# A hybrid flow-matching step: the DRAM round of the triangular blocks in 1 KB pieces on two queues, and small elementwise work moved to GpSimd

## The chip, the cores and the metric

One core of a Trainium2 chip runs the whole program in one launch. The metric is the device time of one execution in microseconds (us), the median of several runs. The core has a matrix engine (TensorE, PE in the profile; its weight loads are PEld), a vector engine (VectorE, DVE), an activation engine (ScalarE, ACT), GpSimd (POOL) and SyncE (SP), whose only work here is to issue DMAs. ScalarE and GpSimd can issue DMAs too. Each engine works through its own instructions in a fixed order and waits on semaphores.

## The reference, cut to what matters

Two layers. Each has four token mixers side by side on 512 latent and 128 context tokens (640 rows, width 1024), which share one input and one output projection, and then a SwiGLU channel mixer.

```python
z = einsum('bld,de->ble', modulated_norm(x), p['w_in'])          # combined input projection
# gated DeltaNet, per chunk of 64 tokens, 4 heads, 2 directions:
a   = where(strict, einsum('nbhid,nbhjd->nbhij', kb, kc) * dmask, 0.0)
sol = lax.linalg.triangular_solve(a + eye(c), rhs, lower=True, unit_diagonal=True)
u, w = sol[..., :dv], sol[..., dv:]
def step(s, xs):                                                 # scan over the chunks
    v_new = u_i - w_i @ s;  o_i = qd_i @ s + qk_i @ v_new
    s = s * gl_i + kd_i.T @ v_new
# GQA: q, k = rms_norm per head, then rope_2d: x*cos + swap(x)*sin
# MLA: q = rms_norm(zcq) @ wq_up;  ckv = rms_norm(zckv);  k_rope = rope_2d(zkr)
x = x + mods[2] * (concat([o_gqa, o_na, o_dn, o_mla]) @ p['w_out'])
x = x + mods[5] * ((silu(h @ w_gate) * (h @ w_up)) @ w_down)
```

All of it is float32. The kernel's products with weights are made of three passes: each weight tile is cast to a rounded form `whi` by ScalarE, and the rest, `wlo = w - whi`, is a subtraction of two tiles in SBUF; the matmuls are `whi*hi`, `whi*lo` and `wlo*hi`.

## The kernel before, in words

A layer is the *mixer* stage (`_Build.mixer`) and then the channel mixer. In the mixer, TensorE's order is written out by a planner (`_Order`): generators `yield` the time from which their next TensorE work may run, and the planner picks by rank. The numbers in `od.via(...)` and `od.now + ...` are the planner's estimates of how long the other engines or a DMA take; nothing else depends on them. The order on the other engines and the DMA queues is set by a scheduler when the program is built.

The planner interleaves two kinds of work. The **filler** is the input projection (tiles `acc` and `tacc`, weights through `weights`, L309) and in layer 0 small `mpart` products for the modulation, whose weights `wmd` come on SP's queue. The **delta chain** (`delta_chain`) is a long chain of small steps: Gram matrices of the keys give 20 blocks of 64x64 per direction (`self.M`, tile `dM`); their diagonal 16x16 blocks are inverted (`inverse16`); from these the 64x64 inverses are put together by TensorE (`inverse`, tiles `ivr`, `invp`, `ivy`); then ten chunks are scanned (`scan`, tiles `ks`, `qs`, `ysp`, `spp`, `opp`), and `delta_out` (tiles `dno`, `otp`) ends it. Only then does the attention begin.

`inverse16` needs another layout: one block per partition instead of one row per partition. So the diagonal blocks go **through DRAM** (`dinv`): eight DMAs write them (L1025, pieces of 64 bytes), two loads bring one direction each into `ivx` and `ivw` (L1034 and L1035, 40 partitions of 4 KB), VectorE transposes one of them (L1037) and does 60 short products and differences on 104 partitions (L1044, L1048), two DMAs write the result back (L1051, L1052) and eight bring it to `rt` (L1055). All 20 are issued by SP. VectorE's copy L1037 waits for the second load, and whatever stands behind it in VectorE's order waits too.

On VectorE there are also: `wlo` of every weight (L309), the copies of `rt` into `dM` (L1128), the last two steps of the GQA rotary (L1441, L1442; GpSimd makes `gsw`, the swapped product, before them), and the scaling of the MLA rows `mcr` (L1552), which are read back from DRAM (`dcraw`) into a single buffer, one of five row blocks at a time.

`wst`, the staging tile of a weight, has three buffers, `whi` and `wlo` two each.

## Time and profile before

| | |
|---|---|
| three runs | 1982.02, 1990.4 and 2092.3 us, median 1990.4 |
| the profiled execution | 1986.23 us, its span 1984.5 us |
| busy in the span | PE 1855.4, DVE 1098.1, ACT 734.1, POOL 282.7 us |
| mean granted TensorE clock | 0.97 of full speed |
| layer 0 | mixer about 45 to 520 us, channel mixer to 1040 us |
| layer 1 | mixer about 1040 to 1480 us, channel mixer to the end |

A row of a chain or a timeline begins with its start in us from the span's start and its length in us. A timeline row with x3 merges three like instructions that follow each other; what stands in brackets is the idle time of the engine before it, and what ended that. The granted clock is a share of full speed (2.4 GHz), averaged over a stretch; at any moment it is full or half.

### The profile page before, as it was taken

To read this page: it belongs to the slowest core of one execution; us is meant where nothing else is said; L and a number is where in the kernel's file an instruction comes from. 1 tells how busy PE (TensorE), PEld (TensorE's weight loads), DVE (VectorE), ACT (ScalarE), POOL (GpSimd) and SP (SyncE) were. 2 spreads that over 40 slices of the span, in tenths; PEclk is the share of its full clock that TensorE was granted. 3 is DMA by queue.
4 is the path that set the end of the run, shared out by engine and by line. 5 is a ranking of instruction groups with operands and counts; after the bars stand their busy time and mean duration, and the time that the engine had idled before them with its cause. 6 is when DMAs were issued, how large, how long until landed. Compare 5 with 4: busy or idle time off the path is not lost.

```text
span 1984.5 us, 40378 instructions
## 1 busy us (share of the span) xinstructions
PE 1855.4 (93%) x16620; PEld 1751.5 (88%) x16620; DVE 1098.1 (55%) x2372; ACT 734.1 (37%) x1505; POOL 282.7 (14%) x470
## 2 busy tenths in 40 slices
PE   5998998899999999999999889789999999999997
PEld 4976787778899999999989889677889999999997
DVE  6464646677657547647555674567765232333344
ACT  4622133766442212222345223277655221221231
POOL 1120312233310000000032131223322000000001
PEclk8998798999999999999999899899999999999999
DMA  7344333132535536435423222223352222222221
GB/s 295 128 114 122 112 94 104 30 108 73 165 130 167 158 99 191 150 113 188 131 89 109 57 76 70 74 56 75 90 172 80 77 78 79 75 67 83 74 96 54
DMA packets 116521, 213.51 MB, mean 108 GB/s; under 512 B 44401, under 2 KB 64369, under 8 KB 116209
## 3 DMA queue, kind: packets, MB, share of 16 engines
q1 hardware_dynamic: 113520, 206.22, 33.3%
q0 software_dynamic: 2816, 4.72, 1.2%
q8 instruction: 130, 2.13, 0.4%
q14 instruction: 55, 0.44, 0.1%
HBM read 186.29 MB, written 19.89 MB: 104 GB/s over the span
## 4 chain that ended last, share of the span: by engine, by line
PE 77%; DVE 8%; DMA 6%; ACT 4%; issue 2%; SPq 2%; POOL 1%; DVEq 0%; ACTq 0%; POOLq 0%
PE acc L351 56%; PE tacc L351 7%; PE ptp L363 2%; PE sc L351 2%; PE pvo L351 2%; PE invp L351 1%; DVE wlo L309 1%; DMA wst<-wout 1%; PE mpart L351 1%; DMA ivw<-dinv 1%; ACT p L1288 1%; ACT whi L308 1%; PE ysp L351 1%; PE spp L351 1%; SPq L1705 1%
## 5 line engine op out<-in xcount | busy, mean ns | idle before, releaser
L351 PE MATMUL acc<-h,whi 128*128 128x256 f32 (+1 forms) x3520 | 685.0, 313 | 2.6 <-ACT h L574 1.4
L351 PEld LDWEIGHTS acc<-h,whi 128*128 128x128 f32 x3520 | 582.6, 190 | 12.4 <-issue 5.1
L308 ACT CAST whi<-wst 128x1024 fp32r<-128x1024 f32 (+3 forms) x210 | 203.6, 970 | 714.6 <-PE acc L351 664.9
L351 PE MATMUL acc<-h,wlo 128*128 128x256 f32 (+1 forms) x1760 | 414.7, 313 | 7.7 <-DVE wlo L309 7.7
L309 DVE TENSOR_TENSOR wlo<-wst,whi 128x1024 fp32r<-128x1024 f32 (+3 forms) x210 | 237.8, 1133 | 210.7 <-ACT whi L308 209.8
L351 PEld LDWEIGHTS acc<-h,wlo 128*128 128x128 f32 x1760 | 322.6, 191 | 10.8 <-DVE wlo L309 8.8
L351 PE MATMUL acc<-g,whi 128*128 128x256 f32 (+1 forms) x1128 | 216.6, 309 | 0.0
L351 PEld LDWEIGHTS acc<-g,whi 128*128 128x128 f32 x1128 | 185.9, 188 | 0.1
L541 POOL TENSOR_TENSOR sq<-sq 128x256 f32<-128x256 f32 (+1 forms) x48 | 48.6, 1012 | 926.2 <-ACT sq L535 925.8
L1806 DVE SCALAR_TENSOR_TENSOR x<-acc,mods,x 128x256 f32<-128x256 f32 (+1 forms) x144 | 55.6, 434 | 186.5 <-PE acc L351 186.4
L507 DVE SCALAR_TENSOR_TENSOR wmj<-wmd,cb 128x1024 f32<-128x1024 f32 x112 | 136.8, 1221 | 39.6 <-DMA wmd<-wmodT 38.4
L351 PE MATMUL tacc<-whi,h 128*128 128x256 f32 (+1 forms) x640 | 149.3, 316 | 1.5 <-ACT whi L308 1.5
L351 PE MATMUL acc<-g,wlo 128*128 128x384 f32 (+1 forms) x564 | 135.2, 309 | 0.0
L351 PEld LDWEIGHTS tacc<-whi,h 128*128 128x128 f32 x640 | 111.5, 195 | 10.5 <-issue 5.0
L351 PE MATMUL acc<-oh,whi 128*128 128x384 f32 (+1 forms) x512 | 115.1, 315 | 1.9 <-DVE xe L1806 1.9
L363 PE MATMUL ptp<-cbase,p 128*128 128x128 f32 x512 | 81.4, 284 | 29.6 <-ACT p L1288 12.3
L351 PEld LDWEIGHTS acc<-g,wlo 128*128 128x128 f32 x564 | 103.2, 188 | 0.0
L351 PE MATMUL tacc<-wlo,h 128*128 128x256 f32 (+1 forms) x320 | 98.9, 309 | 1.8 <-DVE wlo L309 1.8
L363 PEld LDWEIGHTS ptp<-cbase,p 128*128 128x128 f32 x512 | 57.0, 142 | 45.9 <-ACT p L1288 17.1
L2122 DVE TENSOR_TENSOR sg<-acc,sg 128x256 f32<-128x256 f32 x88 | 39.1, 485 | 101.9 <-PE acc L351 101.9
L1288 ACT ACTIVATE p<-sc,sm 128x768 f32<-128x768 f32 (+1 forms) x96 | 79.8, 831 | 33.4 <-DVE sm L1285 23.9
L351 PEld LDWEIGHTS acc<-oh,whi 128*128 128x128 f32 x512 | 84.7, 190 | 4.5 <-PE acc L351 2.4
(322 smaller groups left out, 2624.8 us busy)
## 6 DMA issues: line engine op xcount, KB each, us to landing
wmd<-wmodT SPq DMA_DIRECT2D x56, 512.0 KB, 4.3
wst<-wg SPq DMA_DIRECT2D x44, 512.0 KB, 3.6
wst<-wu SPq DMA_DIRECT2D x44, 512.0 KB, 3.6
wmd<-wmod SPq DMA_DIRECT2D x40, 512.0 KB, 6.6
wst<-wd SPq DMA_DIRECT2D x34, 448.0 KB, 3.7
wst<-wfm SPq DMA_DIRECT2D x24, 512.0 KB, 4.8
wst<-wd SPq DMA_DIRECT2D x16, 512.0 KB, 4.2
wst<-wout SPq DMA_DIRECT2D x28, 256.0 KB, 3.1
```

The source lines that it names most:

```text
L308: self.nc.scalar.copy(hi, src)
L309: self.nc.vector.tensor_tensor(out=lo, in0=src, in1=hi.bitcast(F32), op=ALU.subtract)
L351: self.nc.tensor.matmul(out, lhsT, rhs, start=start, stop=stop)
L363: self.nc.tensor.transpose(out, in_, self.ident)
L507: nc.vector.scalar_tensor_tensor(out=j, in0=st, scalar=1.0, in1=self.cb[:, g], op0=ALU.mult, op1=ALU.mult, accum_out=self.msum[:, e, g:g + 1])
L541: (eng or nc.gpsimd).tensor_tensor(out=self.sq[hf][0], in0=self.sq[hf][0], in1=sq, op=ALU.add)
L1288: nc.scalar.activation(p, s, AF.Exp, bias=m, accum_out=d)
L1705: nc.sync.dma_start(out=u[16 * r:16 * r + 16, j], in_=ap)
L1806: self.nc.vector.scalar_tensor_tensor(out=x_out[:, a:b], in0=o[h][:, a - HB * h:b - HB * h], scalar=m[:, 8 * gate + e, grp:grp + 1], in1=x ...
L2122: nc.vector.tensor_tensor(out=sg[:, s], in0=ou[q], in1=sg[:, s], op=ALU.mult)
```

## The change

In `inverse16` the DRAM tile is laid out as [place q, half r, direction d, block b, 256], so that a block of 16x16 floats (1 KB) is one piece. The eight writes go half to SP's queue and half to ScalarE's (`nc.scalar.dma_start`). Each load of 40 partitions by 4 KB becomes two of 20 partitions by four pieces of 1 KB, and so do the writes back. `weights` has a second way, taken while the mixer's planner runs (`self.aside`): GpSimd instead of VectorE makes `wlo`. GpSimd also makes the copies into `dM`, the last two steps of the GQA rotary, and the scaling of `mcr`. The planner's estimates are changed to match.

```diff
@@ weights
-        self.split(hi, lo, st)
+        if self.aside:
+            nc.scalar.copy(hi, st)
+            nc.gpsimd.tensor_tensor(out=lo, in0=st, in1=hi.bitcast(F32), op=ALU.subtract)
+            self.od.via(("ACT", 0.1 + n / 1200), ("Pool", 0.5 + n / 640))
+        else:
+            self.split(hi, lo, st)
+            self.od.via(("ACT", 0.1 + n / 1200), ("DVE", 0.07 + n / 960))
@@ setup
-            "inv": self.dp.tile([L, 2, 2, 2, 20, 4, 256], F32, name="dinv"),
+            "inv": self.dp.tile([L, 2, 4, 2, 2, 20, 256], F32, name="dinv"),
@@ inverse16
-        for r in range(2):
+        for r, eng in enumerate((nc.sync, nc.scalar)):
             for q in range(4):
                 p = slice(64 * r + 16 * q, 64 * r + 16 * q + 16)
-                nc.sync.dma_start(out=Z[0, r, :, :, q].rearrange("d b (j i) -> j (d b) i", j=16),
-                                  in_=M[p, :, :, 16 * q:16 * q + 16].rearrange("p d b i -> p (d b) i"))
+                eng.dma_start(out=Z[0, q, r].rearrange("d b (j i) -> j (d b) i", j=16),
+                              in_=M[p, :, :, 16 * q:16 * q + 16].rearrange("p d b i -> p (d b) i"))
...
-        nc.sync.dma_start(out=X[0:40].rearrange("p q j i -> p (q j i)"), in_=Z[0, :, 0].rearrange("r b q e -> r b (q e)"))
-        nc.sync.dma_start(out=S[64:104].rearrange("p q j i -> p (q j i)"), in_=Z[0, :, 1].rearrange("r b q e -> r b (q e)"))
-        yield od.now + 9.5
+        def rows(t, d, r):
+            return t[64 * d + 20 * r:64 * d + 20 * r + 20].rearrange("p q j i -> p q (j i)")
+
+        for d, t in enumerate((X, S)):
+            for r in range(2):
+                nc.sync.dma_start(out=rows(t, d, r), in_=Z[0, :, r, d].rearrange("q b e -> b q e"))
+        yield od.now + 8.0
...
+        for d, t in enumerate((V, S)):
+            for r in range(2):
+                nc.sync.dma_start(out=Z[1, :, r, d].rearrange("q b e -> b q e"), in_=rows(t, d, r))
@@ inverse, fourth
-                nc.vector.tensor_copy(M[p, :, a:b, cols[q]], rt[p, :, a:b])
+                nc.gpsimd.tensor_copy(M[p, :, a:b, cols[q]], rt[p, :, a:b])
@@ gqa_norm
-                nc.vector.tensor_tensor(out=x, in0=x, in1=cos.unsqueeze(1).to_broadcast([128, 6, 64]), op=ALU.mult)
-                nc.vector.tensor_tensor(out=x, in0=x, in1=sw.rearrange("p (h d) -> p h d", h=6), op=ALU.add)
+                nc.gpsimd.tensor_tensor(out=x, in0=x, in1=cos.unsqueeze(1).to_broadcast([128, 6, 64]), op=ALU.mult)
+                nc.gpsimd.tensor_tensor(out=x, in0=x, in1=sw.rearrange("p (h d) -> p h d", h=6), op=ALU.add)
@@ mla_norm
-                self.in_turn(nc.vector.tensor_scalar(out=cr[:, a:b], in0=cr[:, a:b], scalar1=r[:, t, q:q + 1], scalar2=None,
-                                                     op0=ALU.mult))
+                nc.gpsimd.tensor_scalar(out=cr[:, a:b], in0=cr[:, a:b], scalar1=r[:, t, q:q + 1], scalar2=None, op0=ALU.mult)
@@ mixer
+        self.aside = True
         od.run()
+        self.aside = False
```

SP's queue at the second half of the round in layer 0, before (`wmd` are modulation weights):

```order
L449 DMA wmd<-wmod 128x1024
L1051 DMA dinv<-ivv 2x20x1024
L1052 DMA dinv<-ivw 2x20x1024
L449 DMA wmd<-wmod 128x1024
L1055 DMA rt<-dinv 16x40x16 x8
```

and with the change (`mcr` and `dlat` belong to the MLA rows):

```order
L317 DMA wst<-wfm 128x1024 x2
L1065 DMA dinv<-ivv 20x4x256 x2
L1065 DMA dinv<-ivw 20x4x256 x2
L1548 DMA mcr<-dcraw 128x416
L1550 DMA mcr<-crope 128x2x32
L456 DMA wmd<-wmod 128x1024
L1578 DMA dlat<-mst 128x3x128
L1579 DMA dlat<-mst 32x128
L1068 DMA rt<-dinv 16x40x16 x8
```

The writes back are four, and the load of the next `mcr` now stands behind them and ahead of the loads of `rt`.

VectorE in layer 1, where the copy L1037 waits for the load, before:

```order
L988 TENSOR_TENSOR dM<-gram,dQ 128x2x256
L309 TENSOR_TENSOR wlo<-wst,whi 128x1024
L733 TENSOR_SCALAR convy<-convin,pcol 128x643
L735 SCALAR_TENSOR_TENSOR convy<-convin,pcol,convy 128x643 x3
L1037 COPY ivx<-ivw 40x1024
L1044 TENSOR_TENSOR ivw<-ivv,ivx 104x2x15 x2
```

and GpSimd in the same place with the change:

```order
L1050 COPY ivv<-cbase 128x1024
L734 MEMSET convin 128x4
L324 TENSOR_TENSOR wlo<-wst,whi 128x1024 x3
L734 MEMSET convin 128x1
L734 MEMSET convin 128x3
L734 MEMSET convin 128x4
L324 TENSOR_TENSOR wlo<-wst,whi 128x1024
```

The `wlo` no longer stand in the queue of the engine that waits for the loads; five of them follow GpSimd's filling of `ivv` before the next scaling of `mcr`, in either layer.

TensorE at the end of layer 1's scan, before:

```order
L351 MATMUL ks<-st,qk 64x64 x8
L351 MATMUL qs<-st,qk 64x64 x8
L351 MATMUL otp<-cbase,dno 64x64 x8
L351 MATMUL ysp<-xt,dM 64x64 x8
L351 MATMUL otp<-cbase,dno 64x64 x8
L351 MATMUL spp<-ysb,kd 64x64 x8
L351 MATMUL opp<-ysb,dQ 64x64 x8
L351 MATMUL otp<-cbase,dno 64x64 x16
L351 MATMUL sc<-gk,qst 128x512 x2
```

and with the change:

```order
L358 MATMUL spp<-ysb,kd 64x64 x8
L358 MATMUL acc<-h,whi 128x256
L358 MATMUL acc<-h,whi 128x384
L358 MATMUL opp<-ysb,dQ 64x64 x8
L358 MATMUL acc<-h,wlo 128x256
L358 MATMUL acc<-h,wlo 128x384
...
L358 MATMUL acc<-h,wlo 128x256
L358 MATMUL acc<-h,wlo 128x384
L358 MATMUL otp<-cbase,dno 64x64 x16
L358 MATMUL sc<-gk,qst 128x512 x2
```

Filler (`acc`, 20 of them after the last `opp`) now stands between the last steps of the scan, where before there was none.

## Rows read from the trace of the kernel before

**Rows 1.** The page: busy us of each engine, share of the span, instructions.

```profile
PE 1855.4 (93%) x16620; PEld 1751.5 (88%) x16620; DVE 1098.1 (55%) x2372; ACT 734.1 (37%) x1505; POOL 282.7 (14%) x470
```

**Rows 2.** Windows: stretch, width, busy us by engine (instructions), granted clock, DMA share, GB/s.

```profile
112.00:182.00 70.00, 57.84 (x630) 52.13 (x629) 40.00 (x113) 16.37 (x34) 1.75 (x10) 0.89 0.46 125
182.00:262.00 80.00, 74.27 (x1321) 62.92 (x1323) 40.63 (x109) 17.45 (x45) 20.16 (x38) 0.82 0.40 121
...
1100.00:1160.00 60.00, 52.49 (x414) 51.15 (x413) 41.06 (x122) 19.57 (x43) 0.35 (x6) 0.91 0.30 76
1160.00:1250.00 90.00, 84.82 (x1773) 76.66 (x1771) 50.52 (x127) 25.66 (x63) 24.01 (x50) 0.96 0.23 72
1250.00:1312.00 62.00, 43.67 (x622) 37.64 (x618) 39.60 (x110) 24.91 (x49) 13.15 (x26) 0.83 0.23 69
```

**Rows 3.** Chain of waits, layer 0's round, then layer 1's: start, us, what.

```profile
119.62 2.58 DMA dinv<-dM
...
123.08 8.96 DMA ivw<-dinv
...
162.91 8.15 DMA dinv<-ivw
...
1106.63 8.90 DMA ivw<-dinv
```

**Rows 4.** Timeline of SP: the eight writes of layer 0's round.

```profile
113.91 6.22 SPq L1025 DMA_DIRECT2D dinv<-dM  x8
```

**Rows 5.** Windows again, while the two loads of layer 0 alone run.

```profile
130.00:133.00 3.00, 0.39 (x3) 0.13 (x1) 0.86 (x1) 0.00 (x0) 0.00 (x0) 1.00 0.13 52
```

**Rows 6.** DMA issues: form, count, KB each, median us to landing.

```profile
nck<-nkT SPq DMA_DIRECT2D x16, 64.0 KB, 3.0
```

**Rows 7.** Timeline of VectorE: start and end of layer 0's `inverse16`.

```profile
132.14 1.03 DVE L1037 COPY ivx<-ivw 40x1024 f32<-40x1024 f32 x1 [5.68 <-DMA ivw<-dinv]
...
161.81 1.08 DVE L1050 COPY ivw<-ivv 40x1024 f32<-40x1024 f32 x1
```

**Rows 8.** TensorE's waits in four stretches: who, for whom, us, times, longest.

```profile
PE mpart L351 <- DVE ivw L1044: 4.3, 1, 4.3
PE invp L351 <- DVE ivr L1081: 4.1, 1, 4.1
...
PE invp L351 <- DVE ivr L1081: 3.0, 1, 3.0
...
PE acc L351 <- DVE wlo L309: 6.9, 2, 6.2
...
PE invp L351 <- DVE ivr L1081: 5.1, 2, 4.9
PE otp L351 <- DVE dno L1263: 8.0, 2, 5.6
PE ks L351 <- DVE st L1225: 3.2, 2, 2.8
```

**Rows 9.** GpSimd by form: shapes, count, busy us, mean ns, idle before and releaser.

```profile
L584 POOL TENSOR_TENSOR h<-nt,h 128x384 fp32r<-128x384 f32 x16 | 16.7, 1045 | 48.3 <-ACT nt L578 48.3
L966 POOL TENSOR_TENSOR decay<-cbase,fg 128x512 f32<-128x512 f32 x10 | 12.9, 1315 | 8.1 <-DVE fg L931 8.1
L584 POOL TENSOR_TENSOR h<-nt,h 128x256 fp32r<-128x256 f32 x16 | 12.9, 806 | 47.3 <-ACT nt L578 45.8 <-PE acc L351 1.5
```

**Rows 10.** VectorE by form, 40 to 520 us: the same columns.

```profile
L309 DVE TENSOR_TENSOR wlo<-wst,whi 128x1024 fp32r<-128x1024 f32 x18 | 22.2, 1232 | 23.2 <-ACT whi L308 23.2
```

**Rows 11.** Timelines of VectorE and GpSimd, side by side in layer 0.

```profile
96.46 0.68 DVE L967 TENSOR_TENSOR decay<-cbase,gc 128x512 f32<-128x512 f32 x1
97.69 2.98 DVE L967 TENSOR_TENSOR decay<-cbase,gc 128x512 f32<-128x512 f32 x2
97.58 3.99 POOL L966 TENSOR_TENSOR decay<-cbase,fg 128x512 f32<-128x512 f32 x3
```

**Rows 12.** Chain of waits in layer 0, 216 to 226 us.

```profile
218.91 5.16 DMA mcr<-dcraw
```

More of the change, by code (lines that the diff above doesn't have):

```diff
@@ L320, in weights @@
             n *= d
-        self.od.via(("ACT", 0.1 + n / 1200), ("DVE", 0.07 + n / 960))
+        if self.aside:
[5 more added lines that the diff above has]
+            self.od.via(("ACT", 0.1 + n / 1200), ("DVE", 0.07 + n / 960))
         return hi, lo
@@ L903, in gates @@
         nc.vector.tensor_scalar(out=self.lf, in0=m[:, 1], scalar1=-1.0, scalar2=None, op0=ALU.mult)
-        yield od.via(("DVE", 1.6), ("ACT", 2.2), ("DVE", 0.5)) + 4.0
+        yield od.via(("DVE", 1.6), ("ACT", 2.2), ("DVE", 0.5)) + 2.0
         yield "dn", 1
@@ L1050, in inverse16 @@
         nc.vector.tensor_copy(S[64:104], V[64:104].rearrange("p q j i -> p q i j"))
-        nc.sync.dma_start(out=Z[1, :, 0].rearrange("r b q e -> r b (q e)"), in_=V[0:40].rearrange("p q j i -> p (q j i)"))
-        nc.sync.dma_start(out=Z[1, :, 1].rearrange("r b q e -> r b (q e)"), in_=S[64:104].rearrange("p q j i -> p (q j i)"))
+        for d, t in enumerate((V, S)):
+            for r in range(2):
+                nc.sync.dma_start(out=Z[1, :, r, d].rearrange("q b e -> b q e"), in_=rows(t, d, r))
         for r in range(2):
@@ L1056, in inverse16 @@
                                   .rearrange("p d b i -> p (d b) i"),
-                                  in_=Z[1, r, :, :, q].rearrange("d b (j i) -> j (d b) i", j=16))
-        yield od.now + 10.0
+                                  in_=Z[1, q, r].rearrange("d b (j i) -> j (d b) i", j=16))
+        yield od.now + 8.0
         return rt
@@ L1440, in gqa_norm @@
                                                 in1=sn[:, a, b].unsqueeze(1).to_broadcast([128, 6, 16]), op=ALU.mult)
-                nc.vector.tensor_tensor(out=x, in0=x, in1=cos.unsqueeze(1).to_broadcast([128, 6, 64]), op=ALU.mult)
-                nc.vector.tensor_tensor(out=x, in0=x, in1=sw.rearrange("p (h d) -> p h d", h=6), op=ALU.add)
-            yield od.via(("DVE", 1.5)) + 2.5
+                nc.gpsimd.tensor_tensor(out=x, in0=x, in1=cos.unsqueeze(1).to_broadcast([128, 6, 64]), op=ALU.mult)
+                nc.gpsimd.tensor_tensor(out=x, in0=x, in1=sw.rearrange("p (h d) -> p h d", h=6), op=ALU.add)
+            yield od.via(("DVE", 0.8), ("Pool", 5.5 if t < 4 else 1.5))
     def gqa_operands(self, l, g, ar, ma, at, ps):
@@ L1549, in mla_norm @@
                 nc.sync.dma_start(out=A["okr"][l], in_=cr[:, 384:416])
-            yield od.now + 6.0
             for q, (a, b) in enumerate(((0, 256), (256, 384))):
-                self.in_turn(nc.vector.tensor_scalar(out=cr[:, a:b], in0=cr[:, a:b], scalar1=r[:, t, q:q + 1], scalar2=None,
-                                                     op0=ALU.mult))
-            yield od.via(("DVE", 0.7)) + 2.0
+                nc.gpsimd.tensor_scalar(out=cr[:, a:b], in0=cr[:, a:b], scalar1=r[:, t, q:q + 1], scalar2=None, op0=ALU.mult)
+            yield od.now + 9.0
             yield "w", 1
@@ L2015, in mixer @@
         od.spawn(attention(), 0)
+        self.aside = True
         od.run()
+        self.aside = False
         for st in stacks[::-1]:
```

## The prediction

> **What bounds the kernel now.** I read the page first: TensorE is busy in 93% of the span [rows 1], so only its idle time and the time that it runs at a reduced clock can be won. Then the windows, to see where these lie. In the five stretches of [rows 2], which hold the delta chain of either layer, TensorE is idle for 12.2, 5.7, 7.5, 5.2 and 18.3 us (width less busy), 48.9 us in all. The granted clock is below 1 in all five; one less the clock, times the width, is 7.7, 14.4, 5.4, 3.6 and 10.5 us, 41.6 us, the most that the full clock throughout could give back. So about 90 us are at stake, 4.6% of the run. Outside these stretches the change does little: the channel mixers keep VectorE for `wlo`, and of the attention's work only some `wlo` of the output projection move.
>
> Then the waits [rows 8], to see who holds TensorE up. From 112 to 182 us it waits 4.3 us for a bank that VectorE has not emptied, since VectorE stands at its copy L1037, which waits for the DRAM loads [rows 7], and 4.1 us for the transposes of `rt`, the end of the round. From 182 to 262 us it waits 3.0 us for `ivr`: VectorE had stood at the scaling of `mcr`, for whose DMA the chain waits 5.16 us [rows 12]. From 1100 to 1160 us a `wlo` of the filler, 6.2 of 6.9 us, is late, again behind L1037. From 1160 us on 5.1 us go to `ivr`, and at the end, 1250 to 1312 us, 8.0 us to `dno` and 3.2 us to `st`, with no filler left. In words: VectorE's fixed order turns waits for DMAs into waits of TensorE, and the chain is so late that in layer 1 the filler runs out.
>
> **The change, part by part.**
>
> *First half of the round.* Before, it takes from the first write at 113.91 us [rows 4] to the copy at 132.14 us [rows 7], 18.2 us. One issue costs 6.22 / 8 = 0.78 us. With four writes on each of two queues the issue takes 3.1 us, the last write lands 2.6 us on [rows 3], three more issues bring the fourth load 2.3 us later. Its landing is unknown. Before, it was 8.96 us [rows 3], and while the two loads ran alone the 16 DMA engines were busy to 0.13, which is two of them, at 52 GB/s [rows 5]. If the pieces stay on two engines, it remains 9. If they spread, the nearest is a 64 KB transfer in rows of 1 KB, 3.0 us [rows 6]; I take that, since it is nearest in size and piece. Sum 3.1 + 2.6 + 2.3 + 3.0 = 11.0 us: 7.2 us sooner (1.2 if the landing does not change).
>
> The Trainium skill ("DMA: Bandwidth & Descriptors", section "Why a DMA increments its semaphore by 16 and not by 1") says that a transfer is split over the largest number up to 16 that divides the outermost sizes of both sides; the old loads have 40 and 2 there, the new ones 20 and 20, so two engines become ten. The two are what the DMA share shows; by the rule and the same 52 GB/s for two engines, 320 KB would take an estimated 1.3 us in place of 6.3.
>
> *Second half.* 8.15 us [rows 3] become 3.0 + two more issues of 0.78 = 4.6 us: 3.6 us sooner. The eight loads of `rt` stay.
>
> *VectorE's part of `inverse16`*, from 132.14 to 161.81 us: the order takes three `wlo` of 1.23 us [rows 10] out of it, 3.7 us. Against this stands GpSimd. One `wlo` costs it, by 806 and 1045 ns for 256 and 384 columns [rows 9], 1045 + 640 x 1.87 = 2240 ns (at most 2 x 1315 = 2630). Three GpSimd instructions of 128x512 and two of VectorE with both inputs in SBUF, side by side, took 3.99 and 2.98 us, 1.49 us for each of VectorE's, which alone takes 0.68 [rows 11]: they take turns. Five `wlo` follow GpSimd's filling of `ivv`; I let three fall on VectorE's work, 6.7 us (0 to 11.2). So this part becomes 3.0 us longer, and `rt` is there 7.2 + 3.6 - 3.0 = 7.8 us sooner, in either layer.
>
> *What TensorE gets of it.* 112 to 182 us: the 4.3 and the 4.1 us go, both being shorter than the 7.2 and 7.8 us before them. A new wait comes: the second `mcr` product needs a load that now stands on SP's queue behind the writes back, so behind the end of `inverse16`; with [rows 12] as upper bound (0 to 5.2) I take 4.0. Of the lost clock I take back half where the gaps ahead of it go, 3.9. Sum 8.3. 182 to 262 us: 3.0 us go, as `mcr` now holds up GpSimd instead; of the clock a third, 4.8: 7.8. 1100 to 1160 us: 6.2 us go, as no `wlo` stands behind L1037; half of the clock, 2.7: 8.9. 1160 to 1250 us: VectorE no longer waits for GpSimd's rotary product, of 5.1 us 4.9; a third of the clock, 1.2: 6.1. 1250 to 1312 us: `st` stood behind a `wlo`, 3.2 us; the 20 `acc` now between the last steps of the scan fill about 20 x 0.17 = 3.4 us of the 8.0; half of the clock, 5.3: 11.9. Together 43.0 us.
>
> *What it costs.* The order has 56 `wlo` moved, each 2.24 - 1.23 = 1.0 us longer; GpSimd, idle for 86% of the span [rows 1], has room for them and for the rotary, scaling and copies. What hides them is that two weights are prepared ahead. The cover is thinner where GpSimd's order puts a wait ahead of a `wlo` (an `mcr` load, `dM` copies), and the small products `kd`, `st` and `dno` of the scan then stand behind a `wlo`. I take one GpSimd instruction's length for every eighth weight, 7 x 2.24 = 15.7 us, between 0 and 56 x 1.0 = 56. ScalarE's four DMA issues (3.1 us per layer) lie beside 37% of busy time; nothing.
>
> Net 43.0 - 15.7 = 27.3 us. Against the profiled execution's own 1986.2 us that is **1959 us**; the median of the three runs, 1990.4, is 4 us above it.
>
> **The rivals.**
>
> *More comes back.* If GpSimd's lateness is hidden and the clock recovers by two thirds (27.7 of 41.6 us, where I took 17.9), the gain is 25.1 + 27.7 = 52.8: 1986.2 - 52.8 = 1933.4, about 1934 us. For it: the clock is at 1 wherever the filler is unbroken. Against it: the stretches of the smallest products, 182 to 262 us, have the lowest clock with only 5.7 us of idle time.
>
> *The turns eat the chain's gain.* All five `wlo` fall on `inverse16`: 11.2 us less 3.7 make it 7.5 longer, and `rt` is 3.3 us sooner at best. Then the 4.1 and the fill at the end (3.4) stay lost and half of the clock's return with them: 43.0 - 7.5 - 8.9 - 15.7 = 10.9, about 1975 us, and with the `ivr` wait of layer 1 kept too, 1980. The Trainium skill ("SBUF — State Buffer", section "Who interferes with whom") speaks for this: a VectorE instruction with two SBUF inputs and a GpSimd instruction that reads SBUF lock each other out for a whole instruction. By [rows 11] that is so here, with 1.49 against 0.68 us.
>
> *The pieces do not spread.* The loads stay at 9 and 8 us; the round gains 1.2 us and `inverse16` loses 3.0. What is left is VectorE's freedom from waits (3.0, 6.2, 4.9, 3.2) and a third of the clock, 13.9: 31.2 - 4.0 - 15.7 = 11.5, about 1975 us. Against it: the smaller pieces and the even split by 20.
>
> *GpSimd is late (slower than before).* Every `wlo` stands in one queue with waits for DMAs, for `rt` and for the scan. With turns of half of VectorE's 0.68 to 1.23 us added, a `wlo` is 1.0 + 0.5 = 1.5 us late; if TensorE feels it on all 56, that is 84 us against 43: about 2027 us. It decides from 43 / 1.5 = 29 of the 56 on. For it: the prepared weights are only two deep. Against it: TensorE waits for `wlo` only where VectorE itself was held up.
>
> **How the numbers follow.** The forecast has 0.46 (1944 to 1974), more coming back 0.20, the turns 0.16, no spread 0.10, late GpSimd 0.08. The range from 1934 to 1992 leaves out late GpSimd and half of the second case. A measurement of this kernel tells about 2% from no change; 2% of 1990.4 is 40 us, so faster means under 1951 us. That takes nearly all of the second case and a quarter to a third of the first: 0.32. Slower, over 2030 us, is half of the last: 0.04. Within 2%: 0.64.
>
> **What the profile will show.** If the steps are right: the chain's `ivx` and `dinv` DMAs at 3 us instead of 9; the copy after the loads 7 us after where it was, counted from the first write; no wait of TensorE for a `wlo` or a bank behind that copy; a clock above 0.9 in all five stretches; VectorE's part of `inverse16` no more than 33 us. Wrong would be: TensorE waiting for GpSimd's `wlo` for over 30 us, VectorE's products of `inverse16` at twice their length, the DMA share still at 0.13 during the loads, or the end of layer 1's scan as empty as before.

## The result, and the profile after

The changed kernel takes 2001.15 us (median of 7 runs, 1997.1 to 2003.44), the kernel before 1989.85 us on the same chip. The ratio is 1.0073, 95% interval 1.005 to 1.0095: slower by 0.7%, which is within 2%, and 42 us above the forecast of 1959 us, outside the range of 1934 to 1992. The profiled execution has a span of 2001.5 us.

The page and the windows of the changed kernel, as in [rows 1, 2]; the third window, in layer 0's attention, is new:

```profile
PE 1862.3 (93%) x16620; PEld 1754.6 (88%) x16620; DVE 1070.0 (53%) x2256; ACT 734.3 (37%) x1505; POOL 437.6 (22%) x586
```

```profile
112.00:182.00 70.00, 56.82 (x490) 50.99 (x486) 38.04 (x100) 18.93 (x43) 19.99 (x27) 0.85 0.50 123
182.00:262.00 80.00, 73.56 (x1560) 62.55 (x1554) 32.35 (x91) 18.60 (x44) 42.95 (x61) 0.96 0.42 131
330.00:430.00 100.00, 75.53 (x637) 64.61 (x637) 55.34 (x112) 62.77 (x149) 25.26 (x41) 0.93 0.26 68
1100.00:1160.00 60.00, 55.06 (x478) 52.16 (x479) 43.95 (x101) 20.15 (x43) 26.06 (x25) 0.94 0.35 83
1160.00:1250.00 90.00, 80.76 (x1656) 72.76 (x1655) 39.36 (x98) 25.43 (x66) 50.22 (x75) 0.87 0.21 63
1250.00:1312.00 62.00, 53.09 (x686) 46.04 (x686) 33.58 (x107) 18.55 (x35) 22.42 (x31) 0.92 0.23 71
```

GpSimd took over 155 us of work, VectorE is busy for only 28 us less. In the five stretches of the prediction TensorE is idle for 42.7 us instead of 48.9, but from 330 to 430 us for 24.5 (before: 18.0, from its busy 82.01). To see where time went I set the n-th TensorE product of each kind in one trace against the same in the other (medians over 20 us). The changed kernel is 4 us ahead at 280 us and 6 at 300 to 320, 10 behind at 400 and 8 to 10 through the channel mixer, 1 ahead at 1180, then 7 behind at 1260, 12 at 1300, 16.5 at the end. So the chain does gain, in both layers, and gives more than that back behind it.

TensorE's waits in the changed kernel, as in [rows 8], from 112 to 182, 330 to 430, 1100 to 1160 and 1160 to 1250 us:

```profile
PE mpart L358 <- DMA wmd<-wmod: 13.2, 3, 10.0
...
PE sc L358 <- ACT p L1301: 13.7, 5, 5.0
...
PE acc L358 <- POOL wlo L324: 1.6, 1, 1.6
...
PE mtp L370 <- POOL mcr L1560: 5.4, 1, 5.4
```

The waits that were to go (a bank behind L1037, a `wlo` of 6.2 us) are gone, though of the 5.1 us for `ivr` in layer 1 3.9 are left, and 4.5 us for VectorE's copy to `msb` are new from 182 to 262 us. In their place stand `wmd` loads, GpSimd's scaling of `mcr`, and in the attention the softmax, with no filler beside it. A low part itself is hardly waited for.

The round in layer 1, SP's and VectorE's timeline of the changed kernel, as in [rows 4, 7]:

```profile
1107.56 2.22 SPq L1032 DMA_DIRECT2D dinv<-dM  x4
...
1114.01 0.33 SPq L1047 DMA_DIRECT2D ivw<-dinv  x1
```

```profile
1116.50 2.98 DVE L1049 COPY ivx<-ivw 40x1024 f32<-40x1024 f32 x1 [0.19 <-DMA ivw<-dinv]
...
1128.31 0.44 DVE L1060 TENSOR_TENSOR ivv<-ivv,ivw 104x96 f32<-104x96 f32 x2
1128.64 2.58 DVE L1056 TENSOR_TENSOR ivw<-ivv,ivx 104x78 f32<-104x78 f32 x2
...
1132.58 1.12 DVE L1062 COPY ivw<-ivv 40x1024 f32<-40x1024 f32 x1
```

The kernel before, in the same layer:

```profile
1115.62 1.02 DVE L1037 COPY ivx<-ivw 40x1024 f32<-40x1024 f32 x1 [8.11 <-DMA ivw<-dinv]
...
1140.75 1.09 DVE L1050 COPY ivw<-ivv 40x1024 f32<-40x1024 f32 x1
```

From the first write to the copy it takes 8.9 us. The copy takes 2.98 us where it took 1.02, and of a pair of products one is stretched: 2.58 us for the two, where the pair in the row above took 0.44. Beside them ran GpSimd:

```profile
1113.27 5.28 POOL L324 TENSOR_TENSOR wlo<-wst,whi 128x1024 fp32r<-128x1024 f32 x2 [5.32 <-ACT whi L323]
1125.84 5.29 POOL L324 TENSOR_TENSOR wlo<-wst,whi 128x1024 fp32r<-128x1024 f32 x1 [7.29 <-ACT whi L323]
```

The first row has two low parts in 5.28 us; the single one of the second row takes as long as both. It runs beside VectorE's unbroken row of products, and ends when the one long product ends. Experiments say what this is worth.

The early rows are not all used. In layer 0 of the changed kernel the copy comes 16.0 us after the first write, since a convolution stands ahead of it in VectorE's order; it waits for ScalarE, and its first instruction is stretched as well (2.15 us, 0.55 alone):

```profile
114.04 3.54 SPq L1032 DMA_DIRECT2D dinv<-dM  x4
```

```profile
125.05 2.15 DVE L740 TENSOR_SCALAR convy<-convin,pcol 128x643 f32<-128x643 f32 x1 [9.98 <-ACT convin L737]
...
130.01 1.09 DVE L1049 COPY ivx<-ivw 40x1024 f32<-40x1024 f32 x1
...
152.43 1.04 DVE L1062 COPY ivw<-ivv 40x1024 f32<-40x1024 f32 x1
```

In layer 1 the loads of `rt` are issued from 1135.67 us on, but VectorE transposes the first of `rt` 23.3 us later (before: 7.4 us later), behind three convolutions:

```profile
1135.67 4.15 SPq L1068 DMA_DIRECT2D rt<-dinv  x8
```

```profile
1159.00 0.76 DVE L1094 STREAM_TRANSPOSE ivr<-rt 128x256 f32<-128x256 f32 x2
```

### The profile page after: what moved, and what is told of

It reads as the page before. It is cut to its first block, busy times and chain, and to the rows that moved or that the text cites. A ratio compares the mean times of both kernels' runs of the same rounds, so it can differ in the third digit from the quotient of the medians.

```text
span 2001.5 us, 40352 instructions
## 1 busy us (share of the span) xinstructions
PE 1862.3 (93%) x16620; PEld 1754.6 (88%) x16620; DVE 1070.0 (53%) x2256; ACT 734.3 (37%) x1505; POOL 437.6 (22%) x586
## 5 line engine op out<-in xcount | busy, mean ns | idle before, releaser
L310 ACT CAST whi<-wst 128x1024 fp32r<-128x1024 f32 (+2 forms) x154 | 152.0, 988 | 608.4 <-PE acc L358 587.4
L311 DVE TENSOR_TENSOR wlo<-wst,whi 128x1024 fp32r<-128x1024 f32 (+2 forms) x154 | 177.6, 1154 | 153.4 <-ACT whi L310 152.7
L324 POOL TENSOR_TENSOR wlo<-wst,whi 128x1024 fp32r<-128x1024 f32 (+2 forms) x56 | 120.1, 2146 | 165.2 <-ACT whi L323 129.7
L358 PE MATMUL tacc<-whi,h 128*128 128x256 f32 (+1 forms) x640 | 154.9, 320 | 0.9 <-ACT whi L323 0.6
L358 PEld LDWEIGHTS tacc<-whi,h 128*128 128x128 f32 x640 | 113.3, 196 | 11.3 <-issue 5.8
L1304 POOL TENSOR_SCALAR dg<-cbase,sd 128x128 f32<-128x128 f32 x96 | 58.0, 605 | 186.1 <-DVE sd L1302 164.4
```

The costliest lines, as they stand in the source:

```text
L310: self.nc.scalar.copy(hi, src)
L311: self.nc.vector.tensor_tensor(out=lo, in0=src, in1=hi.bitcast(F32), op=ALU.subtract)
L324: nc.gpsimd.tensor_tensor(out=lo, in0=st, in1=hi.bitcast(F32), op=ALU.subtract)
L358: self.nc.tensor.matmul(out, lhsT, rhs, start=start, stop=stop)
L1304: nc.gpsimd.tensor_scalar(out=dg, in0=self.ident, scalar1=d, scalar2=None, op0=ALU.mult)
```

## The experiments

All times are medians; the kernel before was timed beside each (1986.7 to 1989.6 us).

### The planner: e1_dense

```diff
-        od.spawn(attention(), 0)
+        od.spawn(attention(), 0, True)
```

In the planner's own table layer 0's delta chain ends at 276.5 in the changed kernel and the last filler at 278.8; before, the filler ended at 269.8 and the chain at 276.2. The attention asks for five banks at once. Before, they were free when it asked, and it had them at 277.4. Now the filler still holds some, and each bank that comes free is taken by the first head's tasks, which are spawned as dense and go ahead of a task that is not; the attention has its five at 333.9.

> The changed kernel with one word more: the task attention() is spawned as dense, so that its wait for five banks is served before the units that want one bank each. Theory 1 (a tie in the planner): in layer 0 of the changed kernel the planner lets the projections end 2.3 us after the scan; from then on the units of the first head take each bank as it comes free, the wait for five banks is met only when all of them are over, and TensorE stands alone with one head's softmax, idle for 24.5 us from 330 to 430 us where the kernel before is idle for 14.8. The planner's own layer-0 end moves from 493.9 to 465.4. Expected: 8 to 15 us less than the changed kernel's 2001, so about 1986 to 1993, and the idle time of that stretch back to 15 us. Rival (GpSimd is late or VectorE is slowed by it there): within 3 us of 2001.

Measured: 1990.73 us, ratio 1.0014 (0.9997 to 1.0032), 10.4 us less than the changed kernel. (In that stretch the kernel before is idle for 18.0 us, and not for the 14.8 that the expectation took.) From 330 to 430 us, waits and window of this kernel:

```profile
PE sc L358 <- ACT p L1301: 3.5, 1, 3.5
```

```profile
330.00:430.00 100.00, 84.15 (x713) 72.71 (x708) 62.45 (x125) 69.83 (x164) 29.23 (x47) 0.95 0.29 75
```

So 10.4 us of the loss is an order that tipped over by 2 us in a plan, not a price of any moved operation. Of the kernels that follow, e3, e5 and all that are made from the changed kernel have the attention dense. The kernel before has the same order with and without it; e2 and e4 do without it, and in their plans the attention has its five banks at 279.7 and 272.3, with no such stall.

### The parts alone: e2_round, e3_wlo, e4_small, e5_no_wlo

e2 is the kernel before with the hunks of `setup` and `inverse16` alone; e3 with those of `weights` and `mixer` alone (and e1's line); e4 with those of `inverse`, `fourth`, `gqa_norm` and `mla_norm` alone; e5 is e1 without those of `weights` and `mixer`.

> The kernel before with the DRAM round alone changed (1 KB pieces, writes on two queues, its two new waits in the planner); the weights, the rotary and the scaling stay on VectorE. Theory 1: the round is 7.6 us sooner in its first half, as measured in the changed kernel (first write 114.0, loads landed by 125 us), and nothing of GpSimd's stands in the way: 1970 to 1985. In the changed kernel TensorE waits for 10.0 us at 151 us for a modulation weight whose load stands on SP's queue behind the writes back; in this kernel's order that load stands ahead of them, so that wait should be under 4 us. Rival (the round is not on the path, since TensorE has other work): no change, within 3 us of the kernel before.

> The kernel before with the mixers' low weight parts alone on GpSimd; attention() is dense here too, which by itself leaves the order of the kernel before as it is. Theory 1: the weights cost little in TensorE's waits (3.8 us for wlo in the changed kernel's mixers) but VectorE stands still while GpSimd makes one: same or up to 8 us slower than the kernel before. Rival (late GpSimd is what makes the change slow): over 10 us slower, with TensorE waiting for GpSimd's wlo for over 10 us.

> The kernel before with the rotary product and sum, the scaling of the latent rows and the copies of rt alone on GpSimd; weights and round as before. Theory 1: VectorE no longer stands at the scaling behind a DMA, so the 3.0 and 5.1 us of waits for ivr go: 3 to 12 us faster than the kernel before. Rival (GpSimd's fixed order turns these waits into waits of TensorE for mcr and ar): no change or slower, with a wait of TensorE for GpSimd's mcr as the 5.4 us at 1215 us of the changed kernel.

> The changed kernel without the GpSimd weights (all low parts on VectorE again), attention() dense: round, rotary, scaling and copies of rt remain. Theory 2 (round and small work gain, the weights on GpSimd cost more than both): the ratios of the two parts alone multiply, 0.9965 x 0.9955 = 0.992, about 1974 (1968 to 1980). Rival (both parts remove the same waits): no more than the larger of the two, 1978 to 1983.

| | us | ratio to before | interval |
|---|---|---|---|
| e2_round | 1982.92 | 0.9965 | 0.9946 to 0.9985 |
| e3_wlo | 2014.14 | 1.0136 | 1.0115 to 1.0158 |
| e4_small | 1977.85 | 0.9955 | 0.9937 to 0.9973 |
| e5_no_wlo | 1964.65 | 0.9889 | 0.9861 to 0.9917 |

Round and small work together gain 24.7 us against before (1989.32 in that batch), more than the 6.5 and 11.6 of each, and more than either expectation of e5 said. (e5 also keeps a planner estimate of the change that none of the parts has, 2.0 for 4.0 us ahead of the decays; its share was not tried.) e2 and e4 lie in the ranges that were expected of them, but e2's waits for `wmd` from 112 to 182 us are 8.0 us, the longest 3.7. e3 fits neither of its theories: it is 24.7 us slower, and TensorE waits only 3.8 us for low parts. The low parts on GpSimd cost 26.1 us (1990.73 less 1964.65) beside them, and 24.7 alone. e5 beats both kernels.

The round does what was foretold: SP and VectorE in layer 0 of e2, where SP's first write is at 113.64 us and ScalarE's at 113.27, and VectorE before:

```profile
153.33 0.69 SPq L1058 DMA_DIRECT2D dinv<-ivv  x2
...
156.58 4.14 SPq L1061 DMA_DIRECT2D rt<-dinv  x8
```

```profile
124.97 1.04 DVE L1042 COPY ivx<-ivw 40x1024 f32<-40x1024 f32 x1 [2.92 <-DMA ivw<-dinv]
...
153.29 1.05 DVE L1055 COPY ivw<-ivv 40x1024 f32<-40x1024 f32 x1
163.24 0.77 DVE L1087 STREAM_TRANSPOSE ivr<-rt 128x256 f32<-128x256 f32 x2 [6.21 <-DMA rt<-dinv]
```

```profile
178.12 0.77 DVE L1081 STREAM_TRANSPOSE ivr<-rt 128x256 f32<-128x256 f32 x2 [8.89 <-DMA rt<-dinv]
```

That is 11.3 us from SP's first write to the copy (11.7 from ScalarE's), and `rt` is there 14.9 us sooner than before. TensorE gets 6.5 us of it. Where the rest goes is seen best in e5, matched product by product with before: 14.4 us ahead at 300 us, 7.3 from 440 us on; 31.0 ahead at 1200 us, 21 from 1400 us on. e5's windows, as in [rows 2], and the first wait of the last:

```profile
112.00:182.00 70.00, 59.49 (x613) 52.53 (x613) 38.07 (x107) 18.67 (x43) 9.07 (x22) 0.88 0.52 134
182.00:262.00 80.00, 74.59 (x1517) 62.67 (x1515) 37.41 (x107) 18.92 (x48) 35.20 (x61) 0.98 0.41 127
...
1100.00:1160.00 60.00, 55.46 (x1086) 52.41 (x1085) 47.41 (x131) 21.56 (x50) 28.91 (x39) 1.00 0.34 87
1160.00:1250.00 90.00, 89.43 (x1412) 80.35 (x1399) 41.55 (x124) 24.70 (x61) 30.95 (x59) 0.96 0.20 63
1250.00:1312.00 62.00, 42.28 (x444) 36.01 (x444) 39.69 (x91) 36.99 (x81) 9.63 (x17) 0.89 0.19 56
```

```profile
PE otp L351 <- DVE dno L1269: 8.8, 1, 8.8
```

From 1160 to 1250 us TensorE is idle for 0.6 us; then the filler is used up, and the chain's end stands alone, as empty as before (42.28 busy, [rows 2] 43.67).

In e3, layer 0, GpSimd's and SP's timeline show what a low part does beside `inverse16`:

```profile
144.50 7.90 POOL L323 TENSOR_TENSOR wlo<-wst,whi 128x1024 fp32r<-128x1024 f32 x1 [10.48 <-ACT whi L322]
```

```profile
133.94 18.82 SPq L316 DMA_DIRECT2D wst<-wfm  x2
152.85 0.38 SPq L455 DMA_DIRECT2D wmd<-wmod  x1
```

It takes 7.90 us, SP's queue stands for a weight buffer until it has read the weight, and the `wmd` load, for which TensorE waits 11.54 us from 145.9 on, stands behind.

### The two engines by themselves: e7_probe, e10_probe2

Both are the kernel before with short sections behind it, in each of which GpSimd subtracts 128x1024 beside a row of VectorE instructions; in e10, GpSimd starts later in the row (1.3 to 2.8 us after its first instruction). The diff is e10's.

```diff
+    late = pool.tile([128, 1024], F32, tag="pl", name="pl", bufs=1)
+    nc.scalar.copy(late[:, 0:512], a[:, 0:512])
+    nc.scalar.copy(late[:, 512:1024], a[:, 512:1024])
+    nc.gpsimd.tensor_tensor(out=g, in0=z, in1=late, op=ALU.subtract)
+    fn(a, d)
...
+        for i in range(32):      # "free"; in "chain" in1 is the output before
+            nc.vector.tensor_tensor(out=d[:, 128 * i:128 * i + 128], in0=z[:, 0:128], in1=a[:, 0:128], op=ALU.subtract)
```

> The kernel before, and behind its work seven small sections, each twice: one GpSimd subtraction of 128x1024 from two SBUF inputs, started together with nothing, with 32 VectorE subtractions of 128x128 or 10 of 128x512 from two SBUF inputs, 16 tensor_scalar of 128x512, 12 tensor_reduce of 128x512, 8 subtractions of 128x512 with one input in PSUM, and 6 subtractions with a ScalarE copy between each two. Theory 2: 2.3 us alone; beside the unbroken rows with two SBUF inputs GpSimd gets in only before or after them, so 5 us or more longer, or VectorE's first stands for 2.3 us; beside PSUM inputs and reductions 2.3 us. Rival (they take turns instruction by instruction): GpSimd's is lengthened by about the same share in every row, under 2 times.

> The kernel before with ten short sections behind it, in each of which GpSimd's subtraction of 128x1024 starts about 1.2 us into a row of VectorE's work: none, 32 independent 128x128 subtractions, 32 that depend on each other, inverse16's strided products, twelve of 128x512; each twice. Theory: GpSimd is kept out while VectorE goes from one instruction to the next without a gap, so beside the independent or the strided row its 2.34 us become 5 to 8, and beside the dependent row less. Rival: it always gets in at the next instruction, and it takes 2.3 to 2.5 us in every section, with one VectorE instruction stretched. The time is that of before plus the sections.

Measured: one execution each, 2080.55 and 2078.73 us. In e7 GpSimd took 2.34 to 2.48 us everywhere, and one VectorE instruction beside it was stretched: a subtraction of 128x128 from 0.28 to 2.43 us, of 128x512 from 0.68 to 2.83, a `tensor_scalar` of 128x512 from 0.48 to 2.56; `tensor_reduce` and a subtraction with one input in PSUM stayed at 0.68. e10, GpSimd first, then VectorE beside the first row and beside the second:

```profile
2034.60 7.20 POOL L2196 TENSOR_TENSOR pg<-pz,pl 128x1024 f32<-128x1024 f32 x1 [1.41 <-ACT pl L2194]
2044.29 2.35 POOL L2196 TENSOR_TENSOR pg<-pz,pl 128x1024 f32<-128x1024 f32 x1 [2.48 <-ACT pl L2194]
```

```profile
2034.07 5.54 DVE L2201 TENSOR_TENSOR dfree<-pz,pa 128x128 f32<-128x128 f32 x27
...
2043.33 4.43 DVE L2208 TENSOR_TENSOR dchain<-pz,dchain 128x128 f32<-128x128 f32 x7
```

Beside independent subtractions, which follow each other every 0.2 us, GpSimd stands until the row is as good as over, at 2039.6, and only then does its work: 7.20 us. Beside subtractions that need each other's result it gets in at once, and one of the seven takes 2.47 us. Beside twelve of 128x512 it took 2.81 us, so a row of large ones let it in. The strided row of `inverse16` began after GpSimd was done, and is not tested by this. A hold like the 7.9 us of e3 is thus reproduced once: a row of short VectorE instructions can keep GpSimd out, and where it gets in it keeps one VectorE instruction out for its whole length. It does not always keep it out: beside the same subtractions of 128x128 GpSimd got in at once in e7, and two VectorE instructions of these seven were stretched (the second by GpSimd's next subtraction, at 1989.09):

```profile
1986.31 2.48 POOL L2195 TENSOR_TENSOR gsmall<-pz,pa 128x1024 f32<-128x1024 f32 x1 [1.20 <-ACT pt L2190]
```

```profile
1986.10 5.78 DVE L2204 TENSOR_TENSOR dsmall<-pz,pa 128x128 f32<-128x128 f32 x7
```

What decides between the two is not shown.

### What the 26 us are: e12, e13, e16, e15, e14

All five have e1's plan, so TensorE's order is e1's (but for four products in e12 and e16). e12, e13 and e16 leave the low part out of the sum. e12, and then e13, where f, g and v are `lo`, `st` and `hi` with their columns in one row (`lo = hi` there too; e16 has a second subtraction of 8 columns behind two memsets):

```diff
-            nc.gpsimd.tensor_tensor(out=lo, in0=st, in1=hi.bitcast(F32), op=ALU.subtract)
+            lo = hi                                    # e12; e13 instead:
+            nc.gpsimd.tensor_tensor(out=f[:, 0:8], in0=g[:, 0:8], in1=v[:, 0:8], op=ALU.subtract)
+            for a, b in ((8, n), (8, n), (8, 8 + 3 * n // 8)):
+                nc.gpsimd.memset(f[:, a:b], 0.0)
```

> The changed kernel with its attention dense in the plan (1990.7 us), with the same order on every engine, but without the low parts of the mixers' weights: the high part is used in their place (the low part is left out of the sum), no engine subtracts. Theory A: the 26 us that the low parts on GpSimd cost are time on GpSimd (held ahead of convin and the latents' scaling) and VectorE instructions held beside them; without them 1965 or less. Theory B: they are the order that the planner made because of them; then 1980 or more. Between: both.

> The changed kernel with its attention dense (1990.7 us), with GpSimd's subtraction of each low part replaced by a subtraction of 8 columns, which waits for the same things, and memsets that last as long (2.4 us); the products use the high part twice (the low part is left out of the sum), and TensorE does not wait for the memsets. Theory A, VectorE is held beside the subtraction and GpSimd beside VectorE: memsets neither hold nor are held, the time falls to that without any low part, 1963 to 1972. Theory B, it is GpSimd's own 2.35 us each and what stands behind them in its queue: the time stays at 1983 or more.

> e13 (the memsets in the place of GpSimd's subtraction, 1965.1 us; the low part is left out of the sum) with 8 columns of the weights subtracted before and again behind two memsets, so that the weight buffer is held to the end as by the full subtraction. Theory A (the hold between the two engines is the whole): within 4 us of 1965. Theory C (the late buffers are a good part): 1973 or more.

Measured: e12 1962.91 us, ratio 0.9873 (0.9836 to 0.991); e13 1965.11 us, 0.9875 (0.9856 to 0.9893); e16 1964.63 us, 0.988 (0.9862 to 0.9898). GpSimd's rows in e13:

```profile
L324 POOL MEMSET wlo<- 128x1016 f32 x68 | 64.8, 955 | 1.2
...
L324 POOL TENSOR_TENSOR wlo<-wst,whi 128x8 f32<-128x8 f32 x56 | 19.1, 341 | 121.4 <-ACT whi L323 120.8
```

In e13 GpSimd is busy for 441.1 us in all, in the changed kernel for 437.6: the same load in the same queue, and the 26 us are gone. So it is not GpSimd's time (a wait for `mcr` of 4.1 us is there in e13 too); what is gone is the subtraction that reads SBUF while VectorE does. What e13 lacks beside that is TensorE's wait for the low part itself, 1.6 us in e1. And it has another order: the scheduler, which sees no product wait for a low part, put some 60 of VectorE's 2,100 other instructions, 40 of ScalarE's 1,505 and 27 of SP's 662 transfers in other places than in e1. How much of the 25.6 us that is was not tried by itself. Against much of it speaks that e12, e13 and e16, whose orders differ from each other too, lie within 2.2 us, and that the price goes with the time for which VectorE is held (below, at e6). e16 says that a weight buffer held for 2.6 us costs nothing either; one held for 7.9, as in e3, was not tried by itself. The Trainium skill ("SBUF — State Buffer", section "Who interferes with whom") has it so: a VectorE instruction with two inputs in SBUF collides with a GpSimd instruction that reads SBUF, not with one that only writes. The two runs agree, with 25.6 and 26.1 us between reading and writing; and of 51 VectorE `tensor_tensor` that ran beside a memset of 128x1016 in e13, two were over 0.2 us longer than the median of their tile and shape. A `tensor_scalar` was held beside memsets too, at 59.23 us of e13 (0.55 us alone):

```profile
59.23 2.28 DVE L740 TENSOR_SCALAR convy<-convin,pcol 128x643 f32<-128x643 f32 x1 [5.05 <-ACT convin L737]
```

```diff
-            nc.gpsimd.memset(ci[:, a:b], 0.0)
+            nc.vector.memset(ci[:, a:b], 0.0)          # e15; mla_norm's products on nc.vector too
...
-            nc.gpsimd.tensor_tensor(out=lo, in0=st, in1=hi.bitcast(F32), op=ALU.subtract)
+            for i in range(0, n, n // 4):              # e14
+                nc.gpsimd.tensor_tensor(out=f[:, i:i + n // 4], in0=g[:, i:i + n // 4], in1=v[:, i:i + n // 4], op=ALU.subtract)
```

> The changed kernel with its attention dense (1990.7 us), with the memsets of convin and the rotation and scaling of the mixer latents on VectorE; so TensorE waits for no GpSimd work behind a low part. Theory B (GpSimd's queue): the waits for convin (5.0) and mcr (4.3) go, 6 to 10 us faster. Theory A (the hold): within 3 us, since VectorE stands as long.

> The changed kernel with its attention dense (1990.7 us), each low part on GpSimd in four instructions of a quarter of the columns. Theory A, what counts is how long one VectorE instruction is held (2.4 us at a time, 0.6 with quarters): 5 us or more faster than 1990.7. Theory B, what counts is the sum of the time for which the two engines exclude each other, and four instructions have four starts: within 3 us, or slower.

Measured: e15 1994.06 us, 1.0038 (1.0014 to 1.0061), 3 us more than e1. The waits for `convin` and `mcr` are gone, 4.5 us for low parts themselves stand in the place of the first, and VectorE, with more work, is held more (38 us against 32 in e1, counted as below at e6): GpSimd's queue is not where the 26 us come from. e14 1996.84 us, 1.0046 (1.0029 to 1.0062), 6 us more: theory A falls, shorter holds do not help. That the sum of the exclusion is what counts, theory B's reason, e14 does not show; it shows that GpSimd takes longer. GpSimd's group in e14, and in the changed kernel:

```profile
L324 POOL TENSOR_TENSOR wlo<-wst,whi 128x256 fp32r<-128x256 f32 x136 | 107.8, 824 | 112.9 <-ACT whi L323 92.5 <-ACT og L1921 16.7 <-issue 3.5
```

```profile
L324 POOL TENSOR_TENSOR wlo<-wst,whi 128x1024 fp32r<-128x1024 f32 x34 | 85.6, 2518 | 129.1 <-ACT whi L323 105.2 <-ACT dM L1151 14.1 <-issue 5.2
```

Four quarters take 3.3 us where one took 2.5.

### Attempts to mend it: e6, e8, e9, e11

```diff
+        self.aside = False     # e6, in inverse16 behind the issue of the loads
...
+        self.aside = True      # e6, ahead of the copy before the writes back
-            self.od.via(("ACT", 0.1 + n / 1200), ("Pool", 0.5 + n / 640))
+            self.od.via(("ACT", 0.1 + n / 1200), ("Pool", 2.0 + n / 320))     # e8
-                nc.sync.dma_start(out=st, in_=self.A["wmod"][n, j])
+                nc.scalar.dma_start(out=st, in_=self.A["wmod"][n, j])         # e9
-            yield od.now + 9.0
+            yield od.now + 13.0     # e11, on e5; behind the scaling of mcr
```

> The changed kernel with attention() dense (1990.7), and the weights that are prepared from the first write of the round to the write back made on VectorE again; the others stay on GpSimd. Theory 2: what costs is GpSimd beside VectorE's unbroken row of products in inverse16, where one low part took 7.9 to 8.1 us (2.4 alone) and SP's queue stood behind its buffer: 8 us or more faster than with all of them on GpSimd, 1975 to 1983. Rival (GpSimd's weights are late everywhere, since each is 1 us longer): within 4 us of 1990.7.

> The changed kernel with attention() dense, and the planner told that a low part of 1024 columns takes GpSimd 5.2 us where it was told 2.1; the code that runs is the same, in another order. Rival theory 3 (the order is made for a GpSimd that is quicker than it is): 8 us or more faster than 1990.7. Theory 2 (the shut-out itself costs, whatever the order): within 5 us of 1990.7.

> The changed kernel with its attention dense in the plan (1990.7 us), and the wmd loads of modulation issued by ScalarE instead of SyncE. Theory: SyncE's queue is what makes TensorE wait for wmd (9.81 us at 149.35, 13.3 in 112-182), because the load stands behind loads that are held for a buffer or for VectorE's inverse16. Then the wait in 112-182 falls below 5 us and the kernel gains 5 to 10 us (1981 to 1986). Rival: ScalarE issues late too, or TensorE waits for the next thing instead; the time stays within 3 us of 1990.7.

> The version without low parts on GpSimd (1964.7 us), and the planner's delay before the scaling of the mixer latents raised from 9 to 13 us. Theory: the wait of 6.3 us at 144 behind the scaling goes, since the rows arrive by then and other work stands ahead; 3 to 6 us faster. Rival: TensorE waits for the same rows elsewhere; within 2 us of 1964.7.

e6 1984.2 us, 0.999 (0.9972 to 1.0007), and e8 1984.47 us, 0.9983 (0.996 to 1.0006): each 6 us less than e1, between its theories. e6 keeps the low parts away from `inverse16` and still costs 19.5 us more than e5, so most of the price lies elsewhere. In e1, 19 VectorE instructions that run beside a low part are over 0.7 us longer than the median of their line and shape, 32 us in all; in e6 it is 17 with 24 us, in e8 14 with 25, in e15 26 with 38, in e5 and e12 none. Over e5 these four kernels take 26.1, 19.5, 19.8 and 29.4 us longer: about four fifths of the time for which VectorE is held.

e9 2011.98 us, 1.0129 (1.0097 to 1.0161): the theory fell. At the program's start TensorE waits 31.1 us for the squares of `x`, which ScalarE makes only when its queue is past the `wmd` loads; and in the round the wait for `wmd` stays (9.8 us at 166.33), since ScalarE's queue stands behind VectorE as SP's does:

```profile
171.27 0.63 ACT L758 ACTIVATE convin<-convy 128x512 f32<-128x512 f32 x1 [6.52 <-DVE ivv L1060]
171.71 0.34 ACTq L456 DMA_DIRECT2D wmd<-wmod  x1
```

e11, at 1958.27 us, 0.9862 (0.9827 to 0.9897), has the lowest time. The wait of 6.3 us for `mcr` is gone, but 4.6 us for `wmd` stand in its place; its interval overlaps e5's, so a gain over e5 is not shown.

## Why the prediction was wrong, point by point

Foretold: 43.0 us gained, 15.7 lost. Measured: 24.7 gained (e5), 26.1 lost to the low parts (e1 less e5), 10.4 lost to the planner. Together that is 11.8 us slower (11.3 in the first comparison). The three differences follow each other from one kernel to the next, so their sum is the whole by its making and no check of the parts.

- *The cost of the 56 `wlo`, 15.7 us: this step failed.* It priced them as lateness of GpSimd, one length for every eighth weight. TensorE itself waits 1.9 us for low parts in the changed kernel; what the runs show in its place is a price of 26.1 us for subtractions on GpSimd that read SBUF while VectorE does, and nearly none for the same time in memsets. The two shut each other out; a part of it that lies in the scheduler's order is not excluded. [Rows 11] showed the exclusion, and the prediction used it for three `wlo` in `inverse16` only. A `wlo` beside the convolution, the scan's small work or the copy pays as well (2.15 us for a `tensor_scalar` of 0.55 at 125.05 us).
- *`inverse16` 3.0 us longer: wrong sign.* From copy to copy it takes 22.4 us in layer 0 (130.01 to 152.43; before 29.7) and 16.1 in layer 1 (before 25.1). The filler's VectorE work left it, and only one or two stretched instructions came in.
- *First half 11.0, second 4.6 us: right for the DMAs.* 8.9 us in layer 1 and 11.7 in e2, there by terms that offset each other: the first load is issued after 7.6 us in place of 5.7, three more issues take 1.1 in place of 2.3, and the copy starts 3.0 us after the last, as foretold. In layer 0 of the changed kernel VectorE's order makes 16.0 of it. The second half, from the first write back to the first load of `rt`, took 3.25 us in e2 (153.33 to 156.58) and 4.3 in the changed kernel, with `mcr`, `wmd` and `dlat` between.
- *`rt` there 7.8 us sooner: more in layer 0, less in layer 1.* From the first write to the first transposition it takes 52.9 us (before 64.2) and 51.4 us (before 57.9).
- *The new wait on SP's queue, 4.0 us: the place was right, the load another, the size too small.* 10.0 us for `wmd` at 151.46, whose load stands behind the writes back; the product of `mcr` comes right behind it:

```profile
161.47 1.08 PE L358 MATMUL mpart<-wmd,sc 128*32 128x256 f32 x8 [10.01 <-DMA wmd<-wmod]
```

- *TensorE's 8.3 + 7.8 us in layer 0: right where the low parts are left alone; 8.9 + 6.1 in layer 1: too small.* e5 is 14.4 us ahead at 300 us (16.1 foretold). At 1200 us it is 31.0 ahead, and 31.1 were foretold, but by luck: 7 of the 14.4 were given back in between, and layer 1 won 23.7 in place of 15.0.
- *The clock, 17.9 us back: 7.6 in the changed kernel.* The loss in the five stretches, worked out as in the prediction, falls from 41.6 to 34.0 us, and two of them stay below 0.9 (0.85 and 0.87). In e5 it falls to 20.4, 21.2 back, with 8.1 us less of idle time; these stretches hold somewhat later work there.
- *The 11.9 us at layer 1's end: wrong sign.* From 1250 us on the changed kernel loses 6 us to the kernel before, product by product. The filler is a fixed amount. What it fills earlier is missing later: e5 gives back 7 us in layer 0's attention and 10 behind 1200 us. Order rows showed filler at the end in the changed kernel, and the stretch is fuller by it (53.09 busy, [rows 2] 43.67); but that filler was late, not extra.
- *The planner: not in the prediction.* The order of the attention in layer 0 was not read; its 10.4 us have nothing to do with the engines.

Of the rivals, the turns had the right mechanism and the wrong place; late GpSimd is refuted by e13 and e15, the pieces that don't spread by e2, and of more coming back nothing was seen in the changed kernel, whose clock over the whole run is 0.969, before 0.97.

## What to carry to other kernels

Before work is moved from VectorE to GpSimd, ask what it reads: a GpSimd subtraction from SBUF can cost a VectorE instruction that reads SBUF its whole length where they meet. Here the same work had better stay on the busier engine: 56 subtractions on VectorE (e5, 0.9889 of before) cost hardly more than none at all (e12, 0.9873; the intervals overlap). Work that is sooner gains only while there is filler left to run beside it; add up the filler once, over the whole stage. After a change of planner estimates, compare the order of stages that it doesn't touch.

## What the runs showed of the hardware

- GpSimd can be kept out by a row of short VectorE instructions until the row ends (7.20 us for 2.34 in e10, where none of them is over 0.30 us), but beside the same instructions it also got in at once (2.48 us in e7).
- A `tensor_scalar` with a single SBUF input was stretched too (0.48 to 2.56 us), `tensor_reduce` and a subtraction from PSUM were not.
- GpSimd's memset of 128x1016 takes 0.955 us and leaves VectorE's `tensor_tensor` at their length but for two of 51; a `tensor_scalar` beside memsets was held (2.28 us for 0.55 in e13).
